# Five gates of the first branch moved behind the sparse attention, the query split on VectorE, the compressed layer later, and the program ordered on the framework's other machine model

## The chip, the cores and the metric

The kernel is one program on 1 core of one Trainium2 chip. The time is device microseconds of one execution, and the median of several runs is compared. For the kernel before, three runs gave 914.75, 915.25 and 917.64 us, so the median is 915.25 us. A separate profiled execution took 914.49 us.

## The reference

It is one block of a transformer on 512 positions of width 1024, all in float32, followed by a last RMS norm:

```
u = rmsnorm(x);  p = u @ w_in            # q,k,v of three branches, and the merge gates g
o_a = stick-breaking attention, 4 heads
o_b = sparse attention: index scores choose the 256 best keys of each query
o_c = g0 * compressed + g1 * selected blocks + g2 * window      # gates of their own
h  = x + (sum over branches j of sigmoid(g[j]) * (o_j @ w_up[j])) @ w_out
h += memory attention (256 memory rows);  h += swiglu(rmsnorm(h));  out = rmsnorm(h)
```

The gates g of the merge are 3 x 1024 columns of w_in, so they need only u, which is there early. The compressed part of branch c squeezes 32 positions at a time through a small two-layer network with a gelu ("compressed" below is its second half).

## The kernel before

Every large product is done in a split form: each operand is stored as a rounded high part and a low rest, and three matmuls (`mm3`, L93: high x high, high x low, low x high) add up in PSUM. `split` (L64) makes the pair. By default ACT writes the high part (L60) and DVE subtracts for the low part (L68); a call can name another engine.

Weights come through two rings. `ring` (L73) loads 512 KB into a buffer `raw` (issued on SP), and splits it into `whi` and `wlo`. `load_split` (L90) has three buffers of each kind and subtracts on DVE; `load_fill` (L91) has two and subtracts on GpSimd (POOL).

The stages, in the order of the text: the norm and the projections of branch a; stick-breaking attention (`stick_pair`, L358); the eight merge gates of branch a (`fill_gate(0, f)`, L405), each 24 matmuls over 512 columns from one load of `load_fill`, and `merge_up(0, ...)` (L407), eight products of 6 matmuls that multiply the gates by o_a @ w_up; the projections of branches b and c with the compression (L524 to L549); attention of branch c, four query blocks of three parts each (L617), with the eight gates of branch c (L624) and sixteen rounds of top-k on the index scores (L626, three rows of scores each round), which run on DVE alone; merge of c; sparse attention of branch b (L635) with half of the gates of b; the norm and projection of the memory; then output product, memory attention and feed-forward layer.

The projections work in chunks of 128 rows. `project_chunk` (L222) issues 24 matmuls, ACT copies the result out, and a `post` function makes what follows. For the three query projections `post_q` (L279) rotates the chunk on DVE (five instructions, L244 to L246), ACT casts the high part, and POOL subtracts for the low part (tile `stk`); then TensorE transposes (L253). The transposes of a chunk are held back in a list, `late`, and are queued on TensorE behind the matmuls of the next chunk.

`compressed` (L498) is a chain: ACT copies `hid` out, five small DVE instructions and one on ACT make the gelu (L502 to L508), TensorE transposes (L511), and two more products give the keys `kc` and values `vc` that only `cmp_attention` uses.

The order of the text is not the order of the engines. Tile, the framework, takes the place in the text as a priority, plays the whole program at compile time on a model of the machine, and starts on each engine the first instruction in the text whose inputs and buffers are there at that moment of the model. The order so found is fixed: on the chip every engine runs its own list from front to back, and an instruction that has to wait holds all behind it. `tc.issue_after` adds a rule "behind this instruction in its engine's list". A load waits for a free buffer of its ring, and the model gives a freed buffer to the first in the text that wants one; so a gate written behind `compress` can get a buffer of `load_fill` only when the four weight loads of `compress` (L493) have had theirs.

The first branch's gates are copied raw out of PSUM (L370), and their tanh is done later (L396), behind the last exponential of the stick-breaking stage (`last_exp`); gates of the other branches get their tanh at once (L372). The table of ACT's functions is loaded twice in the trace, at the start and before the first tanh.

Of the kernel before, what the change touches and what calls it, by code (L numbers as in the profile page):

```python
# [18 lines left out]
NK = D // P  # L19
# [7 lines left out]
def block_kernel(ctx: ExitStack, tc: tile.TileContext, A, out, dbg=None):  # L27
    nc = tc.nc
# [5 lines left out]
    def dump(name, ap):  # L34
        if dbg and name in dbg:
            nc.sync.dma_start(dbg[name], ap)
# [21 lines left out]
    def copy(eng, dst, src):  # L58
        if eng is nc.scalar:
            nc.scalar.copy(dst, src)  # L60
        else:
            eng.tensor_copy(dst, src)

    def split(dst_hi, dst_lo, src, hi_eng=None, lo_eng=None, scale=None):  # L64

        if scale is None:
            copy(hi_eng or nc.scalar, dst_hi, src)
            (lo_eng or nc.vector).tensor_sub(dst_lo, src, dst_hi.bitcast(F32))  # L68
        else:
            nc.scalar.activation(dst_hi, src, AF.Copy, scale=scale)  # L70
            nc.vector.scalar_tensor_tensor(dst_lo, src, scale, dst_hi.bitcast(F32), op0=ALU.mult, op1=ALU.subtract)

    def ring(pl, bufs, hi_eng=None, lo_eng=None):  # L73

        def load(shape, parts, lo_eng=lo_eng):
            n = shape[0] * shape[1]
            raw = pl.tile([P, WT], F32, name="raw", bufs=bufs[0])
            rv = raw[:, :n].rearrange("p (k n) -> p k n", n=shape[1])
            off = 0
            for src in parts:  # L80
                w = src.shape[-1]
                nc.sync.dma_start(rv[:, :, off:off + w], src)
                off += w
            hi = pl.tile([P, WT], F32R, name="whi", bufs=bufs[1])
            lo = pl.tile([P, WT], F32R, name="wlo", bufs=bufs[1])
            split(hi[:, :n], lo[:, :n], raw[:, :n], hi_eng, lo_eng)
            return [t[:, :n].rearrange("p (k n) -> p k n", n=shape[1]) for t in (hi, lo)]
        return load

    load_split = ring(stage, (3, 3))  # L90
    load_fill = ring(fill, (2, 2), lo_eng=nc.gpsimd)  # L91
# [13 lines left out]
    def col_view(w, c0, n):  # L105
        return w.rearrange("(k p) n -> p k n", p=P)[:, :, c0:c0 + n]
# [41 lines left out]
    def cc(c):  # L148
        return slice(c * P, (c + 1) * P)
# [4 lines left out]
    gf_ps = pm.enter_context(tc.tile_pool(name="gf_ps", bufs=2, space=PSUM))  # L154
# [14 lines left out]
    def load_half(ranges, k0, kn, load):  # L169
        hi, lo = load((kn, sum(w for _, w in ranges)), [col_view(w_in, c0, w)[:, k0:k0 + kn, :] for c0, w in ranges])  # L170
        return [(hi[:, k, :], lo[:, k, :]) for k in range(kn)]
# [40 lines left out]
    def flush(ins=None):  # L212

        while late:
            f = late.pop(0)
            if f and ins is not None:
                with tc.issue_after(ins):
                    f()
            elif f:
                f()  # L220

    def project_chunk(c, n, tiles, post):  # L222
        acc = gm_ps.tile([P, 512], F32, name=up_tag[gm_ps is gf_ps])
        for k in range(NK):
            ins = mm3(acc[:, :n], (uT[0][:, k, cc(c)], uT[1][:, k, cc(c)]), tiles[k], k == 0, k == NK - 1)
        flush(ins)
        p = pw.tile([P, 336], F32, name="p", bufs=2)
        nc.scalar.copy(p[:, :n], acc[:, :n])
        late.append(post(c, p))

    def project(ranges, kstep, post):
        n = sum(w for _, w in ranges)
        tiles = [t for k0 in range(0, NK, kstep) for t in load_half(ranges, k0, min(kstep, NK - k0), load_split)]
        for c in range(NT):
            project_chunk(c, n, tiles, post)
# [43 lines left out]
    def post_q(dst, scale):  # L279

        def f(c, p):
            r = rope(None, p[:, 0:256].rearrange("p (h a d) -> p h a d", a=2, d=32), c, 4)
            rf = r.rearrange("p h a d -> p h (a d)")
            st = pw.tile([P, 4, 2, 64], F32R, name="stk", bufs=1)
            split(st[:, :, 0, :], st[:, :, 1, :], rf, lo_eng=nc.gpsimd)
            sf = st.bitcast(F32).rearrange("p h a d -> p h (a d)")
            return lambda: transposes([sf[:, h, :] for h in range(4)], [(dst[:, :, cc(c)], slice(0, 4), scale)])
        return f
# [71 lines left out]


    g_t = {}

    def merge_gate(j, f, g, load, bank, cols=slice(0, S)):

        w = load((NK, P), [col_view(w_in, 2128 + j * D + f * P, P)])
        for k in range(NK):
            mm3(bank, [t[:, k, :] for t in w], [t[:, k, cols] for t in uT], k == 0, k == NK - 1)
        if j == 0:
            nc.scalar.copy(g, bank)  # L370
        else:
            nc.scalar.activation(g, bank, AF.Tanh, scale=0.5)  # L372

    def fill_gate(j, f, n=S):
        g_t[j, f] = gp_.tile([P, S], F32, name="g", bufs=16)
        gp = gf_ps.tile([P, 512], F32, name="gf")
        merge_gate(j, f, g_t[j, f][:, :n], load_split if j == 1 and f % 2 else load_fill, gp[:, :n], slice(0, n))

    def load_up(j, fh, load):
        return load((2, 512), [A["w_up"][0, j].rearrange("(k p) n -> p k n", p=P)[:, :, fh * 512:(fh + 1) * 512]])  # L380
# [8 lines left out]
    def merge_up(j, name, load, up_ps, n=S):  # L389
        for f in range(NK):  # L390
            if f % 4 == 0:
                w = load_up(j, f // 4, load)
            g, first = g_t[j, f][:, :n], g_t[0, f][:, :n]
            if j == 0:
                with tc.issue_after(last_exp[0]):
                    nc.scalar.activation(g, g, AF.Tanh, scale=0.5)  # L396
            up = up_ps.tile([P, 512], F32, name=up_tag[up_ps is gf_ps])
            add_up(w, f, name, g, up[:, :n], slice(0, n))
            if j == 1:
                nc.vector.tensor_add(first, first, g)  # L400
                split(mg[0][:, f, :n], mg[1][:, f, :n], first, lo_eng=nc.gpsimd)
            elif j == 2:
                nc.gpsimd.tensor_add(first, first, g)

    for f in range(NK):  # L405
        fill_gate(0, f)
    merge_up(0, "a", load_fill, gf_ps)  # L407
    a_st.close()
    p1.close()

# [87 lines left out]
    def compressed(hid):  # L498
        hs = cw.tile([P, 512], F32, name="rel", bufs=2)
        v, t = hs[0:32, 0:256], hs[0:32, 256:512]  # L500
        nc.scalar.copy(v, hid[0:32].rearrange("p a b -> p (a b)"))
        nc.vector.tensor_mul(t, v, v)  # L502
        nc.vector.tensor_scalar(t, t, 0.044715, 1.0, op0=ALU.mult, op1=ALU.add)
        nc.vector.tensor_mul(t, t, v)
        nc.scalar.activation(t, t, AF.Exp, scale=-1.5957691216057308)
        nc.vector.tensor_scalar(t, t, 1.0, None, op0=ALU.add)
        nc.vector.reciprocal(t, t)
        nc.vector.tensor_mul(v, v, t)  # L508
        tp = ps.tile([P, 512], F32, name="ps")
        for x in range(2):  # L510
            nc.tensor.transpose(tp[:, 32 * x:32 * x + 32], v[:, 128 * x:128 * x + 128], ident[0:32, 0:32])  # L511
        ht = cw.tile([P, 2, 32], F32, name="ht")
        nc.vector.tensor_copy(ht, tp[:, 0:64].rearrange("p (a b) -> p a b", b=32))
        w2t = cw.tile([P, 3, 64], F32, name="w2t")
        for i in range(2):
            nc.scalar.dma_start(w2t[:, i, :], A["cmp_w2_k"][0])
        nc.scalar.dma_start(w2t[:, 2, :], A["cmp_w2_v"][0])
        res = ps.tile([P, 512], F32, name="ps")
        nc.tensor.matmul(res[:, 0:32], w2t[:, 0:2, :].rearrange("p a d -> p (a d)"), ht[:, 0, :], start=True, stop=True)
        nc.tensor.matmul(res[0:32, 64:128], ht[:, 1, :], w2t[:, 2, :], start=True, stop=True)  # L520
        split(kc[0], kc[1], res[:, 0:32])
        nc.vector.tensor_copy(vc, res[0:32, 64:128])
# [4 lines left out]
    hid = av_ps.tile([P, 2, P], F32, name="av")  # L527
# [1 line left out]
    compress(0, blk[0], A["cmp_w1_k"][0], hid)  # L529
    project([(1476, 256)], 4, post_q(qc, 0.125))  # L530
    compress(1, blk[1], A["cmp_w1_v"][0], hid)
    compressed(hid)
    def causal_bias(i):
        return causal[:, S - (i + 1) * P:]


    for i in range(1, NT):
        n = (i + 1) * P
        for h in range(4):
            st = ps.tile([P, 512], F32, name="ps")  # L540
# [6 lines left out]

    qb = bc.tile([P, 4, S], F32R, name="qi")
    project([(768, 256)], 4, post_q(qb, 0.125))  # L549
    flush()  # L550
    pw_st.close()
    cw_st.close()
# [64 lines left out]
    for i in range(NT):  # L617
# [3 lines left out]
        rows_attention(i, qc, kwin, vs["vwin"], causal_bias(i), gates[:, i, 2::3], o_ps, False, True)  # L621
        split(o_c[0][:, :, cc(i)], o_c[1][:, :, cc(i)], o_ps, scale=0.5)
    dump("o_c", o_c[0].bitcast(F32))
    for f in range(NK):  # L624
        fill_gate(2, f)
    for r in range(16):  # L626
# [294 lines left out]
```

## Time and profile before

| | |
|---|---|
| median of 3 runs | 915.25 us (914.75 to 917.64) |
| profiled execution | 914.49 us, of which its instructions span 912.7 us |
| TensorE matmuls (PE) | 860.4 us busy, 94% of the span, 5012 matmuls |
| VectorE (DVE) | 506.0 us, 55% |
| ScalarE (ACT) | 414.8 us, 45% |
| GpSimd (POOL) | 151.3 us, 17% |
| mean granted TensorE clock | 0.988 of full speed |
| DMA | 99.01 MB, mean 108 GB/s |

Busy times of PE include pipelining, so one matmul's listed duration is longer than its share of the stream. "Idle before" is the time an engine sat empty just before an instruction, and the releaser is the work whose end let it go. The core has 16 DMA engines, whose packets are a third busy over the span.

### The profile page before, as it was taken

Reading aid. Unit: us, or ns where it says so; the run is one execution under the profiler, and the core shown is the slowest. Engines: PE = TensorE matmul, PEld = TensorE weight load, DVE = VectorE, ACT = ScalarE, POOL = GpSimd, SP = SyncE. Lnnn points to the kernel's source line nnn. Section 1 sums busy time; section 2 is a strip of 40 time slices with the busy share of each in tenths; the row PEclk is TensorE's granted clock in tenths of the full one; section 3 lists DMA queues with packets and bytes.
Section 4 is the critical chain, followed back from the end, with each engine's and each line's share of the span. In section 5 each row is a group of like instructions: output and inputs, shape, how many; then the busy total and the mean of one; then the engine's idle time right before and its main releaser. Section 6 shows DMA issues by size and latency. Waiting matters only on the chain.

```text
span 912.7 us, 13090 instructions
## 1 busy us (share of the span) xinstructions
PE 860.4 (94%) x5012; PEld 733.2 (80%) x5012; DVE 506.0 (55%) x1143; ACT 414.8 (45%) x784; POOL 151.3 (17%) x128
## 2 busy tenths in 40 slices
PE   5999999987899999889999999999999999999995
PEld 4987879877777677777888879998888888888884
DVE  4466205756799938566778758653334434322226
ACT  6488533453677826444565464442223232221123
POOL 4021244342121162213223020000000000000002
PEclk9999999998999999989999999999999999999998
DMA  9240232343101131456545622653332233322212
GB/s 321 79 108 24 52 93 73 91 116 93 47 25 47 47 92 49 158 182 219 155 140 188 194 80 76 203 162 94 107 101 93 92 93 105 126 92 93 93 47 92
DMA packets 93711, 99.01 MB, mean 108 GB/s; under 512 B 4656, under 2 KB 81616, under 8 KB 93648
## 3 DMA queue, kind: packets, MB, share of 16 engines
q1 hardware_dynamic: 91568, 92.75, 33.5%
q10 hardware_dynamic: 2080, 5.42, 1.8%
q8 instruction: 39, 0.64, 0.3%
q14 instruction: 24, 0.20, 0.1%
HBM read 96.06 MB, written 2.10 MB: 108 GB/s over the span
## 4 chain that ended last, share of the span: by engine, by line
PE 61%; DVE 8%; ACT 2%; issue 1%; DMA 1%; DVEq 0%; ACTq 0%
PE wo L97 9%; PE wo L98 8%; PE wo L96 8%; PE ff L98 4%; PE ff L96 4%; PE ff L97 4%; PE y L98 2%; PE y L97 2%; PE y L96 2%; PE gf L98 2%; PE gf L96 2%; PE gf L97 2%; PE av L103 2%; PE ps L563 1%; PE ps L135 1%
## 5 line engine op out<-in xcount | busy, mean ns | idle before, releaser
L60 ACT CAST whi<-raw 128x1024 fp32r<-128x1024 f32 (+1 forms) x167 | 174.8, 1049 | 287.7 <-PE y L98 78.9
L68 DVE TENSOR_TENSOR wlo<-raw,whi 128x1024 fp32r<-128x1024 f32 (+1 forms) x131 | 164.2, 1255 | 210.5 <-ACT whi L60 210.3
L68 POOL TENSOR_TENSOR wlo<-raw,whi 128x1024 fp32r<-128x1024 f32 x36 | 87.6, 2440 | 281.4 <-ACT whi L60 234.3
L97 PE MATMUL wo<-ut_lo,whi 128*128 128x256 f32 (+1 forms) x320 | 105.3, 329 | 0.0
L98 PE MATMUL wo<-ut_hi,wlo 128*128 128x256 f32 (+1 forms) x320 | 104.6, 327 | 0.0
L96 PE MATMUL wo<-ut_hi,whi 128*128 128x256 f32 (+1 forms) x320 | 104.4, 326 | 0.0
L96 PE MATMUL gf<-ut_hi,whi 128*128 128x512 f32 (+1 forms) x192 | 70.2, 366 | 0.0
L98 PE MATMUL gf<-ut_hi,wlo 128*128 128x512 f32 (+1 forms) x192 | 70.0, 364 | 0.0
L97 PE MATMUL gf<-ut_lo,whi 128*128 128x512 f32 (+1 forms) x192 | 69.8, 364 | 0.0
L96 PE MATMUL ff<-ut_hi,whi 128*128 128x512 f32 (+1 forms) x192 | 67.9, 354 | 0.0
L97 PE MATMUL ff<-ut_lo,whi 128*128 128x512 f32 (+1 forms) x192 | 67.9, 354 | 0.0
L98 PE MATMUL ff<-ut_hi,wlo 128*128 128x512 f32 (+1 forms) x192 | 67.9, 354 | 0.0
L97 PEld LDWEIGHTS wo<-ut_lo,whi 128*128 128x128 f32 x320 | 60.8, 190 | 6.3 <-issue 1.0
L870 POOL TENSOR_TENSOR ut_hi<-ut_hi,ut_lo 128x512 f32<-128x512 f32 x4 | 5.0, 1273 | 367.0 <-ACT ut_hi L869 367.0
L96 PEld LDWEIGHTS wo<-ut_hi,whi 128*128 128x128 f32 x320 | 60.8, 190 | 5.7 <-issue 0.7
L98 PEld LDWEIGHTS wo<-ut_hi,wlo 128*128 128x128 f32 x320 | 60.8, 190 | 5.5 <-issue 0.4
L96 PE MATMUL gm<-whi,ut_hi 128*128 128x256 f32 (+1 forms) x160 | 47.9, 299 | 0.0
L97 PE MATMUL gm<-wlo,ut_hi 128*128 128x256 f32 (+1 forms) x160 | 47.0, 294 | 0.0
L98 PE MATMUL gm<-whi,ut_lo 128*128 128x256 f32 (+1 forms) x160 | 46.6, 292 | 0.0
L98 PEld LDWEIGHTS gf<-ut_hi,wlo 128*128 128x128 f32 x192 | 36.2, 189 | 6.9 <-issue 2.3
L96 PEld LDWEIGHTS gf<-ut_hi,whi 128*128 128x128 f32 x192 | 36.2, 189 | 6.2 <-issue 1.5
L97 PEld LDWEIGHTS ff<-ut_lo,whi 128*128 128x128 f32 x192 | 36.3, 189 | 5.0
(329 smaller groups left out, 2041.4 us busy)
## 6 DMA issues: line engine op xcount, KB each, us to landing
raw<-in_w_ffn_in_dram SPq DMA_DIRECT2D x56, 512.0 KB, 3.6
raw<-in_w_in_dram SPq DMA_DIRECT2D x46, 512.0 KB, 3.9
raw<-in_w_ffn_out_dram SPq DMA_DIRECT2D x22, 512.0 KB, 3.5
raw<-in_w_out_dram SPq DMA_DIRECT2D x16, 512.0 KB, 3.6
raw<-in_w_up_dram SPq DMA_DIRECT2D x8, 512.0 KB, 3.9
xt<-in_x_dram SPq DMA_DIRECT2D x4, 512.0 KB, 9.2
raw<-in_w_mem_kv_dram SPq DMA_DIRECT2D x4, 512.0 KB, 3.7
raw<-in_w_mem_q_dram SPq DMA_DIRECT2D x4, 512.0 KB, 3.8
```

Of the source, the lines that this page charges most:

```text
L60: nc.scalar.copy(dst, src)
L68: (lo_eng or nc.vector).tensor_sub(dst_lo, src, dst_hi.bitcast(F32))
L96: nc.tensor.matmul(dst, lh, rh, start=first, stop=False, skip_group_check=True)
L97: nc.tensor.matmul(dst, lh, rl, start=False, stop=False, skip_group_check=True)
L98: return nc.tensor.matmul(dst, ll, rh, start=False, stop=last, skip_group_check=True).ins
L103: nc.tensor.matmul(dst[64 * x:64 * x + 64], lhs[x], rhs[x], start=first, stop=last, skip_group_check=True)
L135: nc.tensor.transpose(tp[:, k, :], u[:, (4 * b + k) * P:(4 * b + k + 1) * P], ident)
L563: nc.tensor.transpose(tp[0:k, h, :], src[:, h, :], ident)
L870: nc.gpsimd.tensor_mul(yo[:, n], yo[:, n], gain[:, n])
```

## The change

Four things are changed. The low part of the rotated queries is subtracted by the default engine of `split`, DVE, instead of POOL. Of the first branch's eight gates three stay where they were, with copy and later tanh; the other five, and the whole `merge_up(0, ...)`, move behind the attention of branch c and get their tanh straight from PSUM. `compressed(hid)` moves from before the index scores to behind the third query projection. And the context is opened with `schedule_with_timeline_sim=True`, so that the order of every engine's list is found by playing the program on the framework's timeline simulator instead of its default core simulator. This touches the order of all instructions, also where the text is the same.

```diff
@@ post_q
-            split(st[:, :, 0, :], st[:, :, 1, :], rf, lo_eng=nc.gpsimd)
+            split(st[:, :, 0, :], st[:, :, 1, :], rf)
@@ merge_gate
     g_t = {}
+    early_g = 3
...
-        if j == 0:
+        if j == 0 and f < early_g:
             nc.scalar.copy(g, bank)
@@ merge_up
-            if j == 0:
+            if j == 0 and f < early_g:
                 with tc.issue_after(last_exp[0]):
                     nc.scalar.activation(g, g, AF.Tanh, scale=0.5)
@@ behind the stick-breaking attention
-    for f in range(NK):
+    for f in range(early_g):
         fill_gate(0, f)
-    merge_up(0, "a", load_fill, gf_ps)
@@ projections
     compress(1, blk[1], A["cmp_w1_v"][0], hid)
-    compressed(hid)
+
@@ behind the index scores
     project([(768, 256)], 4, post_q(qb, 0.125))
+    compressed(hid)
     flush()
@@ behind the attention of branch c
+    for f in range(early_g, NK):
+        fill_gate(0, f)
+    merge_up(0, "a", load_fill, gf_ps)
     for f in range(NK):
         fill_gate(2, f)
@@ kernel
-    with _tile.TileContext(nc) as tc:
+    with _tile.TileContext(nc, schedule_with_timeline_sim=True) as tc:
```

## Rows read from the trace of the kernel before

**Rows 1.** Busy time by stretch; columns in its first line, (x) counts instructions.

```profile
core 0: us, PE busy (x) PEld busy (x) DVE busy (x) ACT busy (x) POOL busy (x), PEclk, DMA share, GB/s
8.00:101.00 93.00, 87.98 (x579) 78.57 (x580) 53.40 (x110) 65.56 (x146) 12.64 (x5) 1.00 0.37 109
101.00:146.00 45.00, 45.00 (x202) 36.60 (x201) 6.19 (x9) 16.77 (x23) 19.33 (x11) 1.00 0.35 94
146.00:245.00 99.00, 85.20 (x680) 81.43 (x679) 66.38 (x236) 46.61 (x103) 35.88 (x57) 0.97 0.30 82
245.00:320.00 75.00, 74.23 (x431) 53.14 (x430) 71.89 (x267) 57.40 (x141) 12.97 (x6) 1.00 0.16 43
320.00:345.00 25.00, 23.97 (x112) 19.44 (x112) 9.26 (x17) 6.27 (x11) 17.82 (x11) 1.00 0.31 84
345.00:390.00 45.00, 39.20 (x293) 32.86 (x291) 32.94 (x81) 23.56 (x54) 10.54 (x5) 0.99 0.38 117
390.00:570.00 180.00, 172.71 (x1112) 150.31 (x1113) 128.53 (x235) 96.49 (x171) 32.15 (x22) 0.98 0.49 153
570.00:902.00 332.00, 332.00 (x1614) 280.89 (x1613) 130.15 (x171) 97.29 (x128) 1.62 (x2) 1.00 0.33 105
```

**Rows 2.** Who PE waited for, whole span: us in total, times, longest.

```profile
PE ps L135 <- DVE u L131: 8.4, 1, 8.4
PE ps L253 <- POOL stk L68: 6.3, 8, 2.0
PE ps L511 <- DVE rel L508: 5.5, 1, 5.5
PE ps L135 <- DVE h L131: 5.1, 1, 5.1
```

**Rows 3.** Groups by line and shape: the query's subtraction on POOL, 100 to 400 us.

```profile
L68 POOL TENSOR_TENSOR stk<-t,stk 128x256 fp32r<-128x256 f32 x12 | 11.5, 954 | 44.8 <-ACT stk L60 41.3 <-PE gm L98 3.5
```

**Rows 4.** The same view of DVE, 146 to 245 us: an addition of that size.

```profile
L246 DVE TENSOR_TENSOR t<-t,t 128x256 f32<-128x256 f32 x12 | 5.1, 425 | 0.3
```

**Rows 5.** Timeline of DVE, 214.9 to 226.5 us: start, length, [idle before].

```profile
215.41 2.47 DVE L502 TENSOR_TENSOR rel<-rel 32x256 f32<-32x256 f32 x1 [1.74 <-ACT rel L501]
217.91 2.32 DVE L503 TENSOR_SCALAR rel<-rel 32x256 f32<-32x256 f32 x1
220.27 0.41 DVE L504 TENSOR_TENSOR rel<-rel 32x256 f32<-32x256 f32 x1
...
223.29 0.40 DVE L508 TENSOR_TENSOR rel<-rel 32x256 f32<-32x256 f32 x1
```

**Rows 6.** Timeline of POOL, 214 to 226 us.

```profile
215.19 4.90 POOL L68 TENSOR_TENSOR wlo<-raw,whi 128x1024 fp32r<-128x1024 f32 x2 [0.21 <-ACT whi L60]
```

**Rows 7.** Timeline of PE behind that chain.

```profile
223.84 0.39 PE L511 MATMUL ps<-cst,rel 32*128 32x32 f32 x2 [5.54 <-DVE rel L508]
```

**Rows 8.** Busy time in the two stretches of a low granted clock, columns as above.

```profile
222.00:229.00 7.00, 5.16 (x24) 4.89 (x25) 4.71 (x13) 1.72 (x5) 0.00 (x0) 0.52 0.20 60
389.00:396.00 7.00, 5.47 (x17) 4.28 (x18) 4.97 (x7) 3.40 (x10) 0.00 (x0) 0.51 0.57 183
```

**Rows 9.** Groups of PE by line and shape, 101 to 146 us.

```profile
L96 PE MATMUL gf<-ut_hi,whi 128*128 128x512 f32 x46 | 18.2, 397 | 0.0
...
L96 PE MATMUL gf<-o_hi,whi 128*128 128x512 f32 x16 | 6.3, 397 | 0.0
```

**Rows 10.** Groups of POOL by line, 245 to 345 us.

```profile
L68 POOL TENSOR_TENSOR wlo<-raw,whi 128x1024 fp32r<-128x1024 f32 x8 | 19.2, 2396 | 69.6 <-ACT whi L60 69.6
```

**Rows 11.** Timeline of DVE at the memory's norm, 376 to 397 us.

```profile
384.23 2.35 DVE L122 SCALAR_TENSOR_TENSOR rs<-rs 128x1 f32<-128x1 f32 x1
386.61 2.26 DVE L121 SCALAR_TENSOR_TENSOR rs<-rs 128x1 f32<-128x1 f32 x1
388.91 0.16 DVE L122 SCALAR_TENSOR_TENSOR rs<-rs 128x1 f32<-128x1 f32 x1
```

**Rows 12.** Timeline of POOL at the same place.

```profile
383.46 5.40 POOL L68 TENSOR_TENSOR wlo<-raw,whi 128x1024 fp32r<-128x1024 f32 x2 [14.39 <-ACT whi L60]
```

## The prediction, made before the changed kernel ran

> **What bounds the kernel now.** I read the busy shares first, then busy time by stretch, then TensorE's waits, then the single places that those waits name. TensorE has 860.4 us of work in a span of 912.7 us, so it is the bound over most of the kernel, and what can be won is its 52 us of idle time and its slow-clock time. By stretch [rows 1]: from 570 to 902 us, the feed-forward layer, it is never idle, and nothing that the change moves lies there. Of the 21 us at the two ends, before 8 and behind 902 us, the first waits for the norm of x (8.4 us [rows 2]) and the other is the last norm and the stores; I count both as fixed. What is left stands in the middle. 101 to 146 us, the merge gates of the first branch and their products, is the one stretch that is purely TensorE's: 45.0 of 45 us, DVE 6.19. 146 to 245 us, the projections of the other branches, has the largest hole, 99 - 85.2 = 13.8 us. 245 to 320 us, branch c's attention with top-k, is full on TensorE and on DVE at once (74.23 and 71.89 of 75). 320 to 345 us has 1.0 us of idle, 345 to 390 us 5.8, 390 to 570 us 7.3, and 8 to 101 us 5.0.
>
> The list of waits says what the hole from 146 to 245 us is made of [rows 2]: 6.3 us, in eight waits, for POOL's subtraction in the rotated queries, and 5.5 us in one wait for the gelu chain of the compressed layer. The rest of it is 2.0 us.
>
> **The change part by part.** The sum starts from the profiled execution, 914.5 us (912.7 of span and 1.8 around it); the median of the runs is 0.8 us above it.
>
> *The query split.* Twelve subtractions leave POOL, where one takes 954 ns [rows 3], and go to DVE, where an addition of the same size with both inputs in SBUF takes 425 ns [rows 4]. The chain copy, rotation, cast, subtraction, transpose so becomes 0.53 us shorter per chunk. TensorE waits in eight of twelve chunks, 0.79 us on average, so most of the shortening is felt: 8 x 0.53 = 4.2 us. The best case is the whole 6.3 us. On DVE it adds 12 x 0.425 = 5.1 us; in 146 to 245 us DVE is busy 66.38 of 99 us, so that hides under its idle time. If it doesn't, since DVE rotates the next chunk in the same list, the end on the other side is +5.1. I take -4.2, because the row for the DVE form is of the same size and operands.
>
> *The compressed layer later.* Its chain held TensorE for 5.54 us [rows 7], and DVE was not slow by itself: L502 took 2.47 us, L503 2.32 us, and L504, of L502's shape, 0.41 us [rows 5]. The two long ones lie exactly beside two POOL subtractions of weights, 4.90 us in a row [rows 6]. By the Trainium skill, "SBUF — State Buffer", section "Who interferes with whom", an instruction of DVE with two SBUF inputs and one of GpSimd that reads SBUF shut each other out for a whole instruction; the trace agrees on the length, 2.4 us per collision, and by that rule moving the chain pays only where POOL doesn't subtract weights.
>
> Behind the third query projection the chain has other work for TensorE to take: the index scores are done, the window and selection scores don't need it, and five gates are now waiting to be filled in. So I take the wait as gone, 5.5 us. With it should go the half-clock stretch that began while TensorE was empty: from 222 to 229 us the granted clock was 0.52, near the lower of the two levels (1.2 instead of 2.4 GHz), with 5.16 us of busy time [rows 8], which costs half of it, 2.5 us. Together -8.0. The other end is +4.1: the chain meets two collisions again (2 x (2.47 - 0.41)) and holds the first attention of branch c, while wait and clock stay as they were.
>
> *The late gates.* In 101 to 146 us, 202 matmuls take 45.0 us, 0.223 us each [rows 1]; 138 of them are gates and 48 the products (three groups of 46 and three of 16 [rows 9]). Five gates (120) and the products (48) move: 168 x 0.223 = 37.5 us of TensorE work leaves that stretch and comes back behind the attention of branch c. As nothing of it was idle there, removing it wins nothing; it wins only what idle time it fills where it lands, and before 345 us that is 0.8 + 1.0 = 1.8 us. Up to 390 us it would be 7.6, but the gates stand ahead of branch b's attention in the text, so they are used up before. I take -1.8, with -7.6 as the lower end. The weights of seven more loads (five gates, two w_up) are now subtracted on POOL beside that attention, where eight such subtractions of 2.4 us run now [rows 10]. If each blocks a DVE instruction for 2.47 - 0.41 = 2.06 us, that is 14.4 us of DVE, the upper end. I count it at nothing: 37.5 us more of TensorE work lies beside DVE there, and DVE may come late by that much before TensorE runs dry. If that cover were missing the whole 14.4 us would be paid. SP's queue carries the same loads in another order; its ring of two buffers stays with the compression's four loads until these are consumed, so the gates can't come earlier than gates came before. The tanh straight from PSUM saves five ACT copies off the path.
>
> The Trainium skill, "Perfetto Trace Analysis", section "Optimization Strategy", says that interleaving stretches with different busy engines can pay, and 6.19 us of DVE in one stretch against 71.89 in the other looks like its case. By that rule the sum would be taken with the 7.6 us, 895; the rows speak against it, since TensorE is full in both stretches.
>
> *The other machine model.* It can reorder every list, and the trace of before shows nothing of it. What it can win is the idle time that the three other edits don't touch: 5.0 (8 to 101 us), 2.0 (rest of the projections), 5.1 (the memory's norm), 7.3 (390 to 570 us), and half of 5.47 us, 2.7, in the second half-clock stretch [rows 8]: 22 us. What it can lose I bound by the same size. I take 0. One place is likely to change either way: the 5.1 us before the memory's transposes, where two instructions on 128 x 1 took 2.35 and 2.26 us instead of 0.16 [rows 11], again beside two POOL subtractions [rows 12]. Any shift of a few us parts them, or makes such a pair elsewhere.
>
> Sum: 914.5 - 4.2 - 8.0 - 1.8 + 0 = 900.5, and with the 0.8 us up to the median, 901.
>
> **The rivals.**
>
> *A, the new order is better all over.* The collision at the memory's norm goes with its slow clock (5.1 + 2.7), and half of the remaining 14.3 us of scattered idle: 901 - 7.8 - 7.2 = 886. For it: those holes are waits of an in-order list that the model evidently did not foresee, and a model that sees them would put other matmuls there. Against it: two of the largest come from POOL and DVE blocking each other, and nothing says that either model knows that.
>
> *B, the stall comes back.* POOL begins to subtract gate weights as soon as the compression frees the ring, and the chain of the compressed layer now starts then or a little later. If it collides and nothing is queued between, 5.5 + 2.5 us are not won: 909. If instead all seven new subtractions hit DVE on the path, 901 + 14.4 = 915.
>
> *C, nothing that can be told.* The gains and a worse order cancel, within 0.3% of 915.25 (2.7 us, about what a measurement of this kernel can tell from no change): 912.5 to 918.
>
> *D, slower: the transposes of the projections.* 146 to 245 us has twenty chunk ends, each with transposes in TensorE's list that wait for a chain of copy, rotation, cast and split. Where the model takes that chain as shorter than it is, the transposes stand too early and everything behind them waits; the worst of this now is 2.0 us, against 0.79 on average in eight [rows 2]. Another model can put all of them a little earlier: at ten more waits of 2.0 us the time is 921, at twenty 941. It decides from seven on (14 us, the whole gain). For it: no filler for TensorE exists in that stretch, since the ring is held by the compression's loads. Against it: the chain is shorter now, and today's list waits in only eight places.
>
> **How the numbers follow.** The forecast, 901 with a range of its own from 894 to 907, has a chance of 0.42; A 0.20; B (mostly 907 to 912.5) 0.12; C 0.10; D 0.16. Faster by over 0.3% is the forecast, A and B: 0.74; within it C: 0.10; slower D: 0.16. The range goes from 884, which leaves out the better third of A, to 921, which leaves out the worse half of D: about 0.15 outside. It holds B and C, and the part sums with one edit at its bad end (901 + 4.2 + 5.1 = 910 for the split, 901 + 8.0 + 4.1 = 913 for the chain, 915 for the subtractions). The ends of the machine model alone, 879 and 923, lie just outside.
>
> **What would show it.** Split: the wait of L253 falls from 6.3 us to about 2, and its releaser is DVE or ACT. Compressed layer: no wait of several us at L511, the granted clock is 1.0 through the projections, and the DVE instructions at L502 and L503 are short unless a POOL subtraction lies beside them. Late gates: the projections begin near 101 us instead of 146, and a stretch of some 38 us more in which TensorE is full and DVE is not stands between branch c's top-k and branch b's attention. Machine model: 570 to 902 us keeps its length, and the idle time of 8 to 101 and 390 to 570 us stays near 12 us. The prediction is wrong if TensorE's idle time in the projections is not clearly under 8 us, if a new half-clock stretch appears, or if the gain lies mainly in stretches that the first three edits don't touch.

## The result, and the profile after

The changed kernel takes 939.78 us (937.23 to 941.17, four runs) against 915.49 us (914.75 to 917.64, four runs): a ratio of 1.0258 with an interval of 1.0229 to 1.0288. It is 24 us slower; 901 us was forecast, and 921 us was the upper end of the range. The profiled execution was the shortest of the four, 937.23 us, 2.6 us under the median. Source lines of the changed kernel are one higher from 362 to 405 and from 550 to 623, the same as before between, and four higher from 624 on.

The page of the changed kernel, with the granted clock over 40 slices:

```profile
span 935.5 us, 13085 instructions
PEclk9999999999999999798999799799999999999998
```

TensorE is busy for 867.3 us, 6.9 more than before for the same 5012 matmuls, and idle for 68.2 us, 15.9 more. Together that is the 22.8 us by which the span grew. The stages, in the columns of [rows 1]: norm and first projection, stick-breaking attention, projections, query transposes, top-k with the attention of branch c, attention of branch b, memory's norm and products, w_out with memory attention, feed-forward:

```profile
core 0: us, PE busy (x) PEld busy (x) DVE busy (x) ACT busy (x) POOL busy (x), PEclk, DMA share, GB/s
8.00:57.70 49.70, 44.31 (x336) 43.17 (x337) 27.33 (x42) 27.85 (x56) 7.96 (x4) 0.97 0.52 160
57.70:115.80 58.10, 53.49 (x309) 45.60 (x308) 30.68 (x69) 41.15 (x95) 8.83 (x6) 1.00 0.20 56
115.80:185.00 69.20, 69.20 (x596) 68.43 (x596) 58.35 (x212) 35.05 (x81) 22.45 (x44) 1.00 0.36 102
185.00:224.30 39.30, 39.30 (x189) 32.27 (x189) 25.30 (x42) 18.40 (x34) 12.14 (x5) 1.00 0.32 90
224.30:335.20 110.90, 103.60 (x554) 74.56 (x553) 77.81 (x272) 64.39 (x148) 26.39 (x11) 0.97 0.22 59
335.20:384.40 49.20, 45.59 (x304) 36.80 (x304) 33.60 (x79) 21.75 (x52) 17.42 (x11) 1.00 0.29 86
384.40:411.10 26.70, 18.20 (x88) 15.27 (x86) 14.24 (x33) 13.24 (x24) 0.00 (x0) 0.81 0.33 114
411.10:592.50 181.40, 163.55 (x1063) 144.85 (x1063) 124.32 (x227) 90.29 (x159) 31.09 (x22) 0.93 0.49 149
592.50:922.60 330.10, 330.08 (x1584) 279.20 (x1584) 123.36 (x160) 92.83 (x122) 0.00 (x0) 0.99 0.32 99
```

The projections have no idle time any more (115.8 to 224.3 us). The three edits are not the whole reason: ordered by the default model they leave 6.1 us there (86.1 us of TensorE work in the 92.2 us from 108.0 to 200.2 us of the first kernel below), so part of the hole was covered with filler, independent matmuls that can stand anywhere. What was won there is lost behind it, above all from w_out to the feed-forward: 181.4 us, where the kernel before took 162.1 us (411.3 to 573.4). The list of TensorE's waits, answering to [rows 2]:

```profile
PE ps L135 <- DVE u L131: 19.4, 3, 8.5
PE ps L135 <- DVE rs L122: 8.4, 1, 8.4
PE wo L96 <- DVE h L793: 3.1, 1, 3.1
```

One of the three 'u' waits is the start of the kernel (8.5 us, as before); the two others, 6.51 us at 521 us and 4.45 us at 586 us, are new, and both are norms at the end of a memory attention. The 8.4 us is the memory's norm at 392.8 us. About each of them, and about the 3.1 us wait at 440 us, the granted clock is 0.50, the lower of the two levels (1.2 instead of 2.4 GHz). Two more such stretches stand at 19 to 22.5 and 322.5 to 330 us. The four about those waits, in the same columns:

```profile
387.70:398.00 10.30, 5.16 (x20) 4.57 (x21) 6.94 (x21) 6.39 (x15) 0.00 (x0) 0.50 0.24 97
438.90:445.70 6.80, 5.72 (x27) 5.75 (x28) 4.97 (x16) 3.35 (x6) 0.00 (x0) 0.50 0.76 217
517.40:527.70 10.30, 5.64 (x24) 5.02 (x25) 9.68 (x29) 4.44 (x8) 0.00 (x0) 0.50 0.47 145
585.70:595.90 10.20, 7.35 (x32) 6.55 (x33) 5.28 (x10) 2.35 (x4) 0.00 (x0) 0.50 0.00 0
```

### The profile page after: what moved, and what is told of

It is laid out like the page before. It is cut to its first block, busy times and chain, and to the rows that moved or that the text cites. A ratio compares the mean times of both kernels' runs of the same rounds, so it can differ in the third digit from the quotient of the medians.

```text
span 935.5 us, 13085 instructions
## 1 busy us (share of the span) xinstructions
PE 867.3 (93%) x5012; PEld 740.1 (79%) x5012; DVE 525.2 (56%) x1155; ACT 411.0 (44%) x779; POOL 136.2 (15%) x116
## 5 line engine op out<-in xcount | busy, mean ns | idle before, releaser
L68 DVE TENSOR_TENSOR wlo<-raw,whi 128x1024 fp32r<-128x1024 f32 (+1 forms) x131 | 167.0, 1277 | 220.3 <-ACT whi L60 220.0
L96 PE MATMUL wo<-ut_hi,whi 128*128 128x256 f32 (+1 forms) x320 | 106.3, 334 | 3.1 <-DVE h L793 3.1
L96 PEld LDWEIGHTS ff<-ut_hi,whi 128*128 128x128 f32 x192 | 37.1, 193 | 6.8 <-DVE ut_lo L68 1.8
L98 PEld LDWEIGHTS ff<-ut_hi,wlo 128*128 128x128 f32 x192 | 37.0, 193 | 4.9
```

The source lines that it names most:

```text
L96: nc.tensor.matmul(dst, lh, rh, start=first, stop=False, skip_group_check=True)
L98: return nc.tensor.matmul(dst, ll, rh, start=False, stop=last, skip_group_check=True).ins
```

## The experiments

### Which of the four parts costs

Five kernels undo parts: the three text edits without the machine model, the model on the text of before, and the edits one or two at a time.

```diff
# the edits alone: the change without this line; the model alone: this line and nothing else
-    with _tile.TileContext(nc) as tc:
+    with _tile.TileContext(nc, schedule_with_timeline_sim=True) as tc:
```

> The three edits in the text, ordered on the default machine model. Theory M (the other model's order makes the loss, in the memory attention above all): the stretch from the first output product (411 us in both traces) to the feed-forward layer's full stretch is as long as before, 162 us, the second memory chain (its first to its last norm transposes) takes 44 us as before and not 60.5 as after, and the three edits bring their own sum: 901 us, 894 to 907. Rival G (the text edits make the loss, the late gates above all, which shift everything behind them): 930 to 940, with a memory chain near 60 us.

> The text of before, ordered on the timeline simulator. Theory M: the memory stretch is some 19 us longer than before, the second memory chain takes 58 us or more, and the start and the stick-breaking stage lose a few us too: 932 to 945. Rival G: within 5 us of 915, chain near 44 us. A third possibility, that flag and late gates only lose together, would show here as under 920 and in the run of the edits alone as under 910.

> Query split on DVE and compressed layer later, no late gates, default machine model. By the prediction's terms -4.2 and -8.0: 903 us, no half-clock stretch in the projections and no wait of several us at the compressed layer's transposes. By its bad ends (the chain meets POOL's weight subtractions again, DVE's added 5.1 us in front of TensorE): 915 to 924.

> Late gates alone, default machine model. By the prediction's term -1.8: 913 us, between 907 and 929; the projections begin near 101 us instead of 146. If the filled-in gates cover the compressed layer's chain by themselves (they can't if they are loaded too late, as branch c's gates were) it would be 905. If POOL's seven more weight subtractions block DVE on the path, up to 929.

> The kernel before with the query split on VectorE alone, default machine model. The prediction's term for it is -4.2 us, the later compress then -8.0 us; together they measured 908.1 against 914.7, -6.6. If the split's term holds, 910 to 912 us here, and the later compress brings some 2.5 us in place of 8; if the split brings 1 us or nothing (913 to 915 us), the compress brings 5.5 or more.

| kernel | us | ratio to before |
|---|---|---|
| three edits, default model | 907.21 | 0.991 (0.9894 to 0.9927) |
| split and later compress | 908.06 | 0.9921 (0.9903 to 0.994) |
| query split alone | 911.54 | 0.9968 (0.9958 to 0.9979) |
| late gates alone | 914.18 | 0.9988 (0.9977 to 0.9998) |
| model alone | 977.87 | 1.0681 (1.0658 to 1.0704) |

The edits win 7.5 us and the model loses all of it and 24 us more. On the text of before the model costs 63 us, on the edited text 33 us: the edits are worth 7.5 us without it and 38 us with it. The 63 us are well above what I expected. The part that I had in mind came true: from the first matmul of w_out to the feed-forward (452.0 to 633.9 us) it takes 181.9 us in place of 162.1. Most of the rest is in a place that I had not named, top-k and the attention beside it, where TensorE is idle for 35.5 us in the two rows shown next.

### Which edit takes away most of the model's cost

> The kernel before with late gates and the other machine model, without the query split and the later compress. The model cost 63 us on the kernel before (977.9) but only 33 us on the three edits (939.8), so one edit takes away 38 us of its cost. Theory M (the model spends TensorE's filler matmuls early, between the steps of dependent chains, and nothing is left for the stages that wait on VectorE): the late gates do it, because they keep 5 of 8 gates and the up-projection behind the attention. Expected 940 to 950 us, with the top-k starting 35 to 50 us earlier than at 274.5 us. Rival N (the split and the later compress shorten the chain to the last query chunk, and that is what the model reacts to): 968 to 978 us here.

> The kernel before with the query split on VectorE, the later compress and the other machine model, without the late gates. Theory M: 965 to 975 us (the two edits bring some 7 us, as without the model, and the gates are still spent early). Rival N: 940 to 950 us.

Model and late gates took 946.8 us (ratio 1.034, 1.0314 to 1.0365); model, split and later compress 964.74 us (1.0544, 1.0528 to 1.056). The late gates are worth 31 us under the model and 0.6 without it. The traces show why: with them top-k starts at 242.9 us, 31.6 us earlier than in the model alone. First the model alone, its stage from the last query transposes to the end of branch c's attention, in two parts:

```profile
274.40:320.00 45.60, 22.57 (x89) 15.44 (x88) 45.54 (x171) 16.69 (x56) 0.13 (x1) 0.55 0.08 24
320.00:375.80 55.80, 43.32 (x198) 22.65 (x196) 25.07 (x97) 32.08 (x75) 0.00 (x0) 0.72 0.00 1
```

DVE is full for 45.6 us while TensorE has 22.57 us of work, at half clock for most of it, and then DVE has 25 us of work in 55.8. The DMA share (0.08, then 0.00) shows that hardly a weight is loaded here: there is no gate left to compute. They were computed before, as the matmuls on the tile `gf` in the stretch ahead show, between the transposes of the last query chunks (a view of one tile has the columns PE, PEld, DVE and ACT):

```profile
218.20:274.40 56.20, 50.53 (x229) 38.87 (x228) 0.00 (x0) 4.76 (x8) 1.00 0.35 94
```

In every run top-k starts when these transposes end, and not when its input is ready: the last step of the index scores began at 248.2 us here, and DVE then stood idle before its first MAX8 (274.5 us) for 17.0 us, until the transposes:

```profile
its engine sat idle before it (us, times) until:
  PE ps L253: 17.0, 1
```

In the kernel before, the edits alone and the changed kernel the scores' last step began 10.7, 14.9 and 20.1 us ahead of the first MAX8. The scores don't need the last queries; in the text the pool of top-k's small result tile (`mq`) opens only where the pools of the projections close, so a buffer of theirs is the likely reason. No run tests it. So 50 us of filler stood in front of the longest serial chain of DVE. The second half is DVE's own list. The rows of the 48 MAX8 (one per row of scores and round), with first and last start: the kernel before, the edits alone, the changed kernel, the model alone:

```profile
L613 DVE MAX8 m<-score x48: 391/547/691, 245.8 to 316.2; 128x8 f32<-128x256 f32 x16, 128x8 f32<-128x384 f32 x16, 128x8 f32<-128x512 f32 x16
```

```profile
L614 DVE MAX8 m<-score x48: 390/544/692, 200.2 to 276.1; 128x8 f32<-128x256 f32 x16, 128x8 f32<-128x384 f32 x16, 128x8 f32<-128x512 f32 x16
```

```profile
L614 DVE MAX8 m<-score x48: 406/548/697, 224.3 to 281.5; 128x8 f32<-128x256 f32 x16, 128x8 f32<-128x384 f32 x16, 128x8 f32<-128x512 f32 x16
```

```profile
L613 DVE MAX8 m<-score x48: 399/556/694, 274.5 to 330.9; 128x8 f32<-128x256 f32 x16, 128x8 f32<-128x384 f32 x16, 128x8 f32<-128x512 f32 x16
```

On the default model the rounds are spread over 70 to 76 us, with the attention's steps between them, so both finish together. On the other model they fill 56 to 57 us almost alone, and the attention follows. While they run, TensorE lives on filler. The late gates give it filler there; without them it has work for only half of the time.

### Filler kept for the end of a chain

Theory M, from these rows: the other model sets filler between the steps of a chain although the next step is ready, and at the chain's end none is left. The second memory attention shows it. `qT` is the copy of a chunk's transposed queries on DVE, L743 (before: L739) its scores on TensorE; first and last start of both chunks, before and after:

```profile
L739 PE MATMUL ps<-km,qT x16: 376/376/480, 532.1 to 536.9; 64*128 64x256 f32 x16
L731 DVE COPY qT<-ps x2: 424/424/425, 531.6 to 535.5; 128x256 f32<-128x256 f32 x2
```

```profile
L743 PE MATMUL ps<-km,qT x16: 376/376/480, 545.3 to 554.6; 64*128 64x256 f32 x16
L735 DVE COPY qT<-ps x2: 419/422/424, 542.5 to 552.7; 128x256 f32<-128x256 f32 x2
```

Before, the scores began 0.5 us after the first copy had begun; after, 2.8 us, though the copy took 0.42 both times: 24 matmuls of the feed-forward's early pairs (tile `wo`) fill TensorE from 542.3 to 545.3 us. From the first score to the last it is 9.3 us in place of 4.8. At the memory's norm the filler is gate 1, in the tile `gf`. From the last step of branch b's attention on the edits alone have 105 of its matmuls, 12.7 us, to cover the norm; the changed kernel none:

```profile
364.80:377.50 12.70, 12.70 (x105) 12.50 (x105) 0.00 (x0) 1.53 (x4) 1.00 0.50 155
```

```profile
384.40:392.84 8.44, 0.00 (x0) 0.00 (x0) 0.00 (x0) 0.00 (x0) 0.70 0.52 187
```

Four kernels keep filler back in the changed kernel, by a place in TensorE's list alone (shortened; `mo[c]` is the last matmul with w_mem_o of the pair that starts at chunk c, `last_pv[0]` the last matmul of branch b's attention):

```diff
+    with tc.issue_after(mo[2]):                 # last matmul with w_mem_o of the second pair
         ff_pair(early_fp - 1, ...)              # 96 matmuls            (first and second)
+    with tc.issue_after(mo[0]) if cp and k >= 4 else nullcontext():
         mm3(ob[c, half], ...)                   # w_out, 48 matmuls     (second only)
+    with tc.issue_after(last_pv[0]) if f >= 4 else nullcontext():
         fill_gate(1, f, S // 2)                 # 96 matmuls            (third alone); the fourth has all
```

> The changed kernel (939.8 us), with the third early pair of the feed-forward (96 matmuls of 256 columns) queued on TensorE behind the last matmul of the second memory pair's output projection, so that it cannot be spent in the chain before. Nothing else is changed. Theory M: the idle time at the second memory chain's end (4.45 + 0.73 + 1.40 us) and its half-clock stretch (10 us at half speed, worth up to 5 us) go, and no gap as long opens earlier, since there the chain's steps stood ready behind filler: 927 to 933 us. Rival R (the chain of the memory attention is itself longer in this order, by what VectorE and ScalarE do in between, so taking filler out of it only moves the idle time): 937 to 941 us.

> The same, and besides it the second half of the second pair's w_out matmuls (k from 4 on, 64 matmuls of 3 parts at most) queued behind the last matmul of the first pair's memory output projection. Theory M: the idle time at the first chain's end (6.51 + 0.92 us) and its half-clock stretch (517 to 528 us) go as well: 916 to 924 us. Rival R: 937 to 941 us; if only the second hold works, as hold_ff.

> The changed kernel with the last 4 of gate 1's 8 fill gates (96 matmuls of 256 columns, 0.12 us apart) queued on TensorE behind the last matmul of the third attention, where the edits without the model leave 105. Theory M (filler spent between steps that were ready, none left at the chain's end): the 8.40 us wait for the memory norm goes and its half-clock stretch (387.7 to 398.0 us) with it, 928 to 933 us. Rival R (the attention's steps then wait instead, as the memory chain's did in the run that held the feed-forward pair): 937 to 941 us.

> The changed kernel with all three holds (gate 1 behind the third attention, half of the second w_out and the third early feed-forward pair behind the memory projections). If the holds add up: 933.8 - 8 to 11 = 922 to 926 us. If the gate's hold gives nothing: 932 to 935 us.

| held back | us | ratio to before |
|---|---|---|
| nothing (the change) | 939.78 | 1.0258 (1.0229 to 1.0288) |
| feed-forward pair | 938.31 | 1.0243 (1.0219 to 1.0268) |
| and half of w_out | 933.77 | 1.0209 (1.0194 to 1.0224) |
| gate 1 | 936.24 | 1.0217 (1.0192 to 1.0242) |
| all three | 929.42 | 1.0153 (1.0122 to 1.0185) |

All three together win 10 us of the 33 that the model costs, and each less than I expected; the first can't be told from nothing, and the gate's interval still touches that of the changed kernel. So theory M is shown for about a third of the loss. For the feed-forward pair rival R was right: the waits that were removed (4.5 and 0.7 us) came back at other steps, as TensorE's waits from 540 to 603 us in that kernel show:

```profile
PE ff L96 <- DVE ut_lo L68: 3.1, 1, 3.1
PE mm L103 <- ACT ptm L762: 1.9, 1, 1.9
PE mm L96 <- ACT oh L60: 0.7, 1, 0.7
```

The gate's hold shows the mechanism more cleanly in its rows (L137, L294 and L105 there are L135, L292 and L103 of the changed kernel). Its 96 matmuls end the wait for the norm (8.4 to 2.1 us), and branch b's attention, freed of them, ends 42.0 us after branch c's (338.1 to 380.1) in place of 49.2 us (335.2 to 384.4): its steps had stood ready behind filler. But two kinds of waits in it, 0.7 us at the longest in the changed kernel, are now 1.7 and 1.3 us; its waits from 340 to 400 us:

```profile
PE gm L294 <- DVE nm L579: 2.8, 3, 1.7
PE ps L137 <- DVE h L133: 2.1, 1, 2.1
PE av L105 <- DVE pt L62: 2.0, 3, 1.3
```

### Is it TensorE's order alone?

Each instruction has the same name in both programs, so the order that one schedule found can be imposed on the other, with a no-sync edge from each instruction of an engine to the next (shortened). What is not so pinned the model orders anew around it:

```diff
+    for a, b in zip(names, names[1:]):          # names: one engine's instructions in the wanted order
+        tc.add_manual_dep(traced[b], a, NoSync)
```

> The changed kernel, other machine model included, with TensorE's 4910 matmuls held in the order that they have in the three edits without the model (a no-sync edge from each to the one before it); VectorE, ScalarE, GpSimd and the DMA queue are ordered by the other model around it (790 of VectorE's 1107 instructions then stand in the order of the edits without the model, 652 did before). Theory O (the model's cost is the order on TensorE alone: which filler stands between which steps): 905 to 912 us, as the edits alone (907.2). Rival V (the order on VectorE and ScalarE, or on the DMA queue, costs as much): 920 to 940 us.

> The reverse: the three edits on the default machine model, with TensorE held in the order of the changed kernel. Theory O: 932 to 942 us, as the changed kernel (939.8). Rival V: 907 to 920 us.

> The changed kernel with TensorE held in the order of the edits alone only from the first matmul of w_out on (2590 of 4910). The stage from there to the feed-forward's start took 181.4 us in the changed kernel, 163.6 us in the edits alone. Theory O: 918 to 925 us (that stage's 18 us and no more). Rival V: 930 to 940 us.

> The same with TensorE left free and the other four engines held. If the two parts of the loss add up (10.4 us by TensorE, 7.4 us by the others): a stage of 173 to 176 us, 931 to 935 us in all. If the engines' orders are worth something only together, as the 963.3 us of TensorE's order alone in the other model's surroundings suggest: a stage of 180 us or more, 938 to 950 us.

> The changed kernel with all five engines' instructions from w_out on (2584 of TensorE, 389 of VectorE, 252 of ScalarE, 20 of GpSimd, 119 transfers of the SP queue) held in the order of the edits without the model. With TensorE alone so held the stage from w_out to the feed-forward fell from 181.4 to 171.0 us, against 163.6 in the edits alone. If the orders of the other engines hold the remaining 7.4 us: a stage of 163 to 165 us and 918 to 923 us in all. If they do not (the stage is slower for what the stages before leave it: late loads, an idle TensorE): a stage of 168 to 172 us and 925 to 929 us.

| kernel | us | w_out to feed-forward |
|---|---|---|
| changed kernel | 939.78 | 181.4 |
| TensorE in the edits' order, everywhere | 963.25 | 168.2 |
| edits alone, TensorE in the changed kernel's order | 946.4 | 181.7 |
| changed, TensorE in the edits' order from w_out on | 927.97 | 171.0 |
| changed, the four other engines so from w_out on | 944.91 | 185.9 |
| changed, all five so from w_out on | 921.91 | 166.8 |
| edits alone | 907.21 | 163.6 |

Theory O (TensorE alone) fell with the first row: with TensorE in the good order everywhere and the other engines ordered by the model around it, the kernel got 23 us slower still. There top-k ran as a block again (its 48 MAX8 start between 213.4 and 266.5 us), while TensorE's list had the attention's steps early, and TensorE waited for DVE's part of them. The stage, and of that kernel's list of waits the two that are longest in total:

```profile
213.40:324.30 110.90, 84.62 (x422) 58.34 (x421) 75.34 (x270) 57.26 (x139) 14.14 (x6) 0.85 0.09 26
```

```profile
PE gm L292 <- DVE nm L577: 13.0, 11, 2.7
PE ps L564 <- DVE cs L608: 10.8, 2, 6.5
```

The same stage with the same order on TensorE took 72.9 us in the edits alone (200.2 to 273.1). The Trainium skill, "Perfetto Trace Analysis", section "Optimization Strategy", says that interleaving stretches with different busiest engines may help; the two numbers agree with it for top-k and attention, which were interleaved on DVE in the one and not in the other. The second row shows the other side. The edits alone, on the default model, with only TensorE in the changed kernel's order, took 946.4 us (ratio 1.0342, 1.0314 to 1.037), 39 us more than without it, above theory O's 932 to 942 us and far from rival V's 907 to 920. So a worse list on TensorE is enough to lose everything, while a better one by itself doesn't win it back.

From w_out on TensorE's order gives back 10.4 of 17.8 us by itself, the others' order alone costs 4.5 more, and all together give 14.6 us, within 3.2 us of the edits. The stage in the last two rows of the table, all five pinned and the edits alone:

```profile
412.80:579.60 166.80, 159.43 (x1062) 140.99 (x1063) 117.90 (x223) 88.83 (x157) 31.96 (x22) 0.99 0.51 156
```

```profile
402.70:566.40 163.70, 156.92 (x1041) 137.99 (x1040) 117.36 (x216) 87.71 (x154) 29.73 (x19) 0.99 0.49 151
```

So the other engines' lists gain only together with TensorE's, and 14.6 of this stage's 17.8 us are the model's order, shown by putting the other one back.

### A version that beats both

In the edits alone POOL's subtractions still meet DVE at three places: at the memory's norm (two steps of 128 x 1 of 2.39 and 2.27 us beside a pair at 376.13 us, as in [rows 11, 12]), behind the first memory attention (one such step of 2.32 us beside a subtraction at 470.50 us) and, new, at the index scores beside a pair at 172.37 us. The low halves of those loads were given to DVE, the first two places in the first version, the third in the second:

```diff
-        merge_gate(j, f, ..., load_split if j == 1 and f % 2 else load_fill, ...)
+        merge_gate(j, f, ..., load_split if j == 1 and f % 2 else fill_dve if j == 1 and f >= 4 else load_fill, ...)
+        # second version: gate 0's f = 3 and 4 with fill_dve too; fill_dve is load_fill with lo_eng=nc.vector
-            w = load_fill(..., A["w_mem_q"] ...)        # and w_mem_o
+            w = load_fill(..., A["w_mem_q"] ..., lo_eng=nc.vector)
```

> The three edits on the default machine model (907.2 us), with the low halves of three groups of fill loads made on VectorE in place of GpSimd: gate 1's from f = 4 on, w_mem_q's and w_mem_o's (2 + 4 + 4 subtractions at 1.22 us against 2.4 us). In the edits alone the memory norm's two steps of 128 x 1 beside GpSimd's pair at 376.13 us took 2.39 and 2.27 us against 0.16 and 0.21, and TensorE then waited 4.37 us; another 2.26 us wait stands at 474.7 us. If these waits come from the shared port: 900 to 904 us. If VectorE's added 12 us of subtractions stand in the chains themselves: 906 to 912 us.

> The kernel of fast_all (898.5 us), with the low halves of gate 0's fill loads f = 3 and f = 4 on VectorE too. In fast_all GpSimd's pair of them at 172.31 us (4.87 us) stands beside the index scores, whose four steps of 128 x 256 took 1.48 + 3.56 us against some 0.48 each free, and TensorE waits 1.40 and 1.76 us for ScalarE's rel there, with a half-clock stretch behind it (179.8 to 183.2 us). If the port is the cause: 894 to 897 us. If the two subtractions of 1.22 us on VectorE delay the chain as much: 897 to 900 us.

They took 898.49 us (0.9808, 0.9793 to 0.9822) and 896.47 us (0.9802, 0.9789 to 0.9815); the second step can't be told from none by these intervals, though its rows are as expected. The first is below the 900 to 904 us that I expected: the 4.4 us wait at the memory's norm is gone (0.9 us is TensorE's longest wait from 364 to 400 us), and the steps of 128 x 1 there take 0.22 us at most. DVE at the index scores in the edits alone, then in the second version:

```profile
173.54 1.48 DVE L544 SCALAR_TENSOR_TENSOR score<-rel,wi,cst 128x256 f32<-128x256 f32 x1 [1.75 <-ACT rel L543]
175.14 3.56 DVE L544 SCALAR_TENSOR_TENSOR score<-rel,wi,score 128x256 f32<-128x256 f32 x3
```

```profile
172.40 2.36 DVE L68 TENSOR_TENSOR wlo<-raw,whi 128x1024 fp32r<-128x1024 f32 x2 [0.52 <-ACT whi L60]
174.68 0.48 DVE L548 SCALAR_TENSOR_TENSOR score<-rel,wi,cst 128x256 f32<-128x256 f32 x1
175.27 1.67 DVE L548 SCALAR_TENSOR_TENSOR score<-rel,wi,score 128x256 f32<-128x256 f32 x3
```

The same two subtractions, 2.36 us on DVE where they took 4.88 us on POOL, leave the scores at 0.5 us. These are the fastest kernels here, some 2% under the one before, without the other model.

## Why the prediction was wrong

**The step that failed** is "The other machine model. [...] What it can lose I bound by the same size. I take 0." It cost 33 us on this text and 63 us on the old one. The bound was the fault, not only the value. Idle time that is left bounds what a new order can win. What it can lose is the idle time that filler now covers, and that was in the rows: from 245 to 320 us TensorE and DVE were both full [rows 1], and without gates beside it, and with top-k as a block, that stage took 101.4 us with 65.9 us of TensorE work in the run of the model alone. I read full engines as a place where nothing could happen.

**Against the edits alone** the changed kernel's span is 29.9 us longer: 8.4 us before w_out; 17.8 us from w_out to the feed-forward; 1.4 us in the feed-forward, which begins at half clock; 2.4 us in the last norm and stores. Ahead of w_out TensorE's idle time grew by 3.7 us in the norm and first projection (a 2.8 us wait, with the half-clock stretch at 19 us), 2.2 in the stick-breaking attention, 6.0 in top-k with branch c's attention and 5.0 in branch b's attention and the memory's norm, and shrank by 6.1 in the projections; some 25 of its matmuls had moved behind the start of w_out. Only 14.6 of the 17.8 us were given back by an experiment that put the other order back.

**Query split**, -4.2: right in kind, -3.4 measured (911.54 against 914.95; by the interval -3.8 to -1.9). In the edits alone the wait of L253 fell from 6.3 us to 1.7, released by DVE, as forecast, and 426 ns was DVE's median in the changed kernel against the 425 taken.

**Compressed layer later**, -8.0: mis-sized by more than half. The wait at L511 is gone in all kernels that have the edit, and in the changed kernel L502 took 0.41 us. But with the split it gave -6.7, so some 3 to 4 are its own: the pair of subtractions moved to the index scores, where TensorE waited 3.5 us in three pieces, and the half-clock stretch came with it (175.3 to 182.2 us in the edits alone). It was rival B's mechanism at another chain; half of its price was paid.

**Late gates**, -1.8: measured -0.6 (by the interval -2.1 to -0.2), within its bounds; the 14.4 us that DVE might have lost did not show. Their worth under the model, 31 us, came from nothing that I had weighed.

**Rival D**, slower, had 0.16 and a price of 921 to 941, which holds 939.8, but that is luck, since it names the wrong place: the transposes of the projections wait for nothing in the changed kernel. The mechanism is also the reverse of the one it named. Steps were not queued too early; filler was queued ahead of steps that were ready, and the waits came at the ends of chains in other stages.

**The signs that I named** worked in part: no L511 wait, a projection stage without idle time, a feed-forward of its old length (330.1 against 328.7 us from its first matmul at 573.4 to 902.1 us). The sign for the machine model failed: the idle time that was to stay near 12 us is 10.0 us from 8 to 115.8 and 17.9 us from 411.1 to 592.5 us. "A new half-clock stretch" was named as what would make the prediction wrong, and there are four more (six ahead of the last norm in place of two).

**A slip in the sums:** the two ends of the span that the prediction counts as 21 us are 18.7 us (8.0 and 10.7). No term rests on it.

**Open:** what in the other model makes it choose so (a shorter filler, a longer chain, or the order in which it breaks ties) stays open, and so does the part of the loss outside the pinned stage, the 8.4 us before w_out among it.

## What to carry to other kernels

Bound a reordering from both sides with different rows: the gain by the idle time that is left, the loss by the waits that filler covers now, which a profile shows as full engines. When an engine lives on filler beside a chain, count how much of it is left at the chain's end, and keep it there by a place in the list; then look which steps of the chain it had covered before. A schedule is one set of lists: one engine's list from a better schedule can make the kernel worse than either (963 us here, against 940 and 907) or give back a part (10 of 18 us in one stage), so an order is judged only with the lists of all engines.

## What the runs showed that I had not expected

The low clock beside the long waits is a cost of its own: the kernel before has 13.6 us at half clock ahead of its last norm, the changed one 47.8 us, and TensorE is busy 6.9 us longer for the same number of matmuls. And POOL's subtraction does not lengthen every DVE instruction beside it: in the edits alone a MAX8 of 128 x 512 took 0.68 us whether one ran beside it or not, while a step of 128 x 1 went from 0.16 to 2.39 us. The Trainium skill, "SBUF — State Buffer", section "Who interferes with whom", tells the two apart by their inputs: at most one in SBUF does not contend, outside DVE's 2-port perf modes, and two do. For these two the trace agrees. The number of inputs is not all of it, though: L503, with one, took 2.32 us beside POOL's subtraction [rows 5, 6] and 0.28 us in the edits alone, where none ran beside it; whether it was in such a mode no run shows.
